# Sparse attention loop: TensorE's matmuls written in one fixed order, with a lag of two pieces and the projections as filling

## The chip, the cores and the metric

The kernel runs on one core of a Trainium2 chip. The metric is the device time of one execution in microseconds (us), lower is better; the time of a kernel is the median of its runs. The engines are called as in the profile: PE (TensorE), DVE (VectorE), ACT (ScalarE), POOL (GpSimd) and SP (SyncE, which issues most DMAs).

## The reference, cut to what matters

The program is two transformer blocks in float32 on 512 tokens of width 1024. The change touches the attention of the first block's second layer: 16 heads of 64 in 4 groups that share keys and values, and three branches per head (compressed, selected and window) that are weighted by gates and added. With 512 tokens all 8 blocks are selected and the window reaches back over all tokens, so the selected and window branches are both plain causal attention, with different keys and values.

```python
def nsa_attention(q, gates, k_cmp, v_cmp, k_sel, v_sel, k_win, v_win, rel_bias):
    ...
        p_c = jax.nn.softmax(logit_c, axis=-1) * has_any[None, :, None, None, None]
        o_c = jnp.einsum('bqghn,bngd->bqghd', p_c.astype(v_cmp.dtype), v_cmp)
        ...
        p_s = jax.nn.softmax(logit_s, axis=-1)
        o_s = jnp.einsum('bqghk,bqgkd->bqghd', p_s.astype(vs.dtype), vs)
        ...
        p_w = jax.nn.softmax(logit_w, axis=-1)
        o_w = jnp.einsum('bqghk,bkgd->bqghd', p_w.astype(vw.dtype), vw)
        o = gt[..., 0:1] * o_c + gt[..., 1:2] * o_s + gt[..., 2:3] * o_w
...
    return o.reshape(B, S, N_HEADS * HEAD_DIM) @ w_o
```

## The kernel before

Every float32 operand is split into a high and a low part, and a product is three matmuls (high by high, high by low, low by high). The weights stream in as chunks of 512 KB in a fixed order (`Stream`). `take` hands out the next 128x128 tile; at every fourth tile `pre` asks for what is three half chunks ahead: a load on SP's queue (`w`), the high part on ACT (`whi`), and the low part (`wlo`) from DVE, POOL or, where an earlier stage left it in DRAM (`dlo`), by one more load on SP's queue. The buffers are 2 for `w` and 4 for each part, so a load waits until the matmuls of an older half chunk are done.

`nsa` is the attention. Its loop goes over 32 *pieces*: piece n is head n // 2, and the selected branch if n is even, the window branch if it is odd. Each piece has two halves:

- `br_a` makes the scores in four blocks of query rows (`s`, 512, 384, 256 and 128 columns wide, two matmuls each, in 2 banks). DVE adds the bias and takes the minimum, ACT takes the exponential, and at the end DVE makes a factor per row and POOL multiplies the four blocks by it (`pa`, `pb`, `pc`).
- `br_b` turns the weights in three *turns* of 4, 3 and 3 transposes (`pt`, 2 banks); after each, ACT makes the high part `ph` and DVE the low part `pl`, and the *products* with the values follow (`o`, two matmuls per key block).

Each head ends with `cmp_b`, the compressed branch (4 transposes, ACT `ct`, one product, then ACT and DVE `of`, and after the second head of a pair ACT `oh` and DVE `ol`). Between the pieces stands *filling*, a generator per group of 8 pieces (`fill`). In groups 0 to 2 it holds the next group's key and value projection (`kvsteps`), its query projection (`qsteps`) and its compressed scores (`cmp_a`, matmuls `mm<-q,kz`); group 0 first has the compression of keys and values (`phi`, matmuls `mm<-whi,eh`, a small product with much weight). In group 3 it holds the output projection of the first heads (`w_o`, matmuls `mm<-oh,whi`, `mm<-ol,whi`, `mm<-oh,wlo`). The projections' ends work on DVE and ACT: `kvsteps` makes `kf`, `vf`, two `kl` and `vv`, `qsteps` two `qf` and four `q`. The keys are copied to the other half of the partitions by four DMAs on SP's queue (`kh`, `kl`) before the first score matmul.

The program text runs `br_b` three pieces behind `br_a` (`LAG`) and takes 4, 2 or 1 steps of filling per piece (`RATE`). It is not the order on the engines: a scheduler in the kernel's framework takes the text's order as a priority and lists each engine's instructions by when its own costs say that they are ready. Each engine then runs its list in order and waits for semaphores.

## Time and profile before

| | |
|---|---|
| median of 3 runs | 2427.35 us (2426.93 to 2428.57) |
| the profiled execution, its own time | 2430.19 us |
| its span, first to last instruction | 2428.4 us |
| mean granted clock of PE | 0.991 |
| attention loop, with the end of the output projection | from about 613 to 915 us of the span |

The profile records every instruction of one execution. A busy share counts the time in which an engine has at least one instruction open; PE's instructions overlap, so that its pace is better read from the distance between the starts of two matmuls. PEld is PE's loading of weights. Times in the rows are us from the start of the span, means of a group are in ns.

### The profile page before, as it was taken

How to read it: one execution, taken by the hardware profiler on the slowest of the kernel's cores; microseconds unless marked ns; L12 is line 12 of the kernel's file. 1: busy time of each engine (PE TensorE's matmuls, PEld its weight loads, DVE VectorE, ACT ScalarE, POOL GpSimd, SP SyncE). 2: the span in 40 equal slices, each digit the busy share in tenths (PEclk: the TensorE clock that was granted, in tenths of full speed). 3: DMA queues.
4: the chain of work that ended last, by engine and by line, in shares of the span. 5: the costliest groups of instructions: out<-in, count | busy, mean ns of one | idle time of the engine just before them, and what ended most of it. 6: DMA issues, size and time to landing. Idle time of an engine off the chain costs nothing.

```text
span 2428.4 us, 38996 instructions
## 1 busy us (share of the span) xinstructions
PE 2360.5 (97%) x14369; PEld 2070.6 (85%) x14369; DVE 1644.6 (68%) x3260; ACT 1235.7 (51%) x2431; POOL 475.9 (20%) x664
## 2 busy tenths in 40 slices
PE   8999999999999989999999999999999999999997
PEld 6788888887787768888889999998989999998995
DVE  6558757765667778647658884678975567764864
ACT  4235444444777664434545775556554334432442
POOL 1231111122233331111232222123321000000001
PEclk9999999999999999999999999999999999999998
DMA  4666777776743447777766446644456262233232
GB/s 164 179 164 211 259 267 261 262 269 203 232 133 94 127 139 259 267 251 266 264 229 191 123 150 183 187 140 155 148 158 188 96 202 88 88 96 95 89 96 70
DMA packets 156396, 427.40 MB, mean 176 GB/s; under 512 B 23131, under 2 KB 29531, under 8 KB 156155
## 3 DMA queue, kind: packets, MB, share of 16 engines
q1 hardware_dynamic: 119680, 296.15, 38.2%
q0 software_dynamic: 35392, 127.49, 16.3%
q8 instruction: 113, 1.85, 0.3%
q10 hardware_dynamic: 1132, 1.26, 0.2%
q14 instruction: 79, 0.65, 0.1%
HBM read 349.01 MB, written 83.29 MB: 178 GB/s over the span
## 4 chain that ended last, share of the span: by engine, by line
PE 83%; DVE 8%; ACT 4%; DMA 3%; issue 2%; SPq 0%; DVEq 0%; ACTq 0%
PE mm L312 72%; PE g L312 3%; PE o L312 3%; DMA L<-csd 2%; PE s L312 2%; PE pt L316 1%; PE u L316 1%; DVE e L746 1%; ACT L L1566 1%; DVE cvt L1353 1%; PE u L312 1%; DVE pl L321 1%; DVE Ml L321 1%; ACT ph L320 1%; DMA w<-in_ws_dram 0%
## 5 line engine op out<-in xcount | busy, mean ns | idle before, releaser
L312 PE MATMUL mm<-hh,whi 128*128 128x258 f32 (+2 forms) x2464 | 796.1, 324 | 14.6 <-ACT hh L360 6.7
L312 PE MATMUL mm<-hh,wlo 128*128 128x258 f32 (+2 forms) x2464 | 798.5, 324 | 0.0
L312 PE MATMUL mm<-hl,whi 128*128 128x258 f32 (+2 forms) x2464 | 795.8, 323 | 2.4 <-DVE hl L361 2.4
L312 PEld LDWEIGHTS mm<-hh,whi 128*128 128x128 f32 x2464 | 464.7, 189 | 57.6 <-ACT hh L360 9.6
L312 PEld LDWEIGHTS mm<-hl,whi 128*128 128x128 f32 x2464 | 465.3, 189 | 44.1 <-DVE hl L361 3.5
L312 PEld LDWEIGHTS mm<-hh,wlo 128*128 128x128 f32 x2464 | 465.8, 189 | 38.2 <-issue 1.7
L214 ACT ACTIVATE whi<-w 128x512 fp32r<-128x512 f32 x346 | 218.3, 631 | 435.5 <-PE mm L312 334.9
L216 DVE TENSOR_TENSOR wlo<-w,whi 128x512 fp32r<-128x512 f32 x344 | 242.3, 705 | 191.7 <-ACT whi L214 184.6
L312 PE MATMUL mm<-b,whi 128*128 128x512 f32 (+1 forms) x699 | 273.5, 391 | 0.0
L312 PE MATMUL mm<-a,wlo 128*128 128x512 f32 (+1 forms) x699 | 273.5, 391 | 0.0
L312 PE MATMUL mm<-a,whi 128*128 128x512 f32 (+1 forms) x699 | 273.0, 391 | 0.0
L214 ACT ACTIVATE whi<-ax 128x512 fp32r<-128x512 f32 x154 | 97.3, 632 | 211.1 <-PE mm L312 206.2
L178 POOL DMA_DIRECT2D dlo<-al x112 | 60.5, 540 | 543.8 <-DVE al L177 414.0
L216 DVE TENSOR_TENSOR wlo<-ax,whi 128x512 fp32r<-128x512 f32 x154 | 105.9, 687 | 85.8 <-ACT whi L214 85.5
L312 PEld LDWEIGHTS mm<-b,whi 128*128 128x128 f32 x699 | 131.7, 188 | 29.8
L312 PEld LDWEIGHTS mm<-a,wlo 128*128 128x128 f32 x699 | 131.7, 188 | 29.8
L312 PEld LDWEIGHTS mm<-a,whi 128*128 128x128 f32 x699 | 131.7, 188 | 29.7
L207 ACT ACTIVATE whi<-w 128x512 fp32r<-128x512 f32 x182 | 111.8, 623 | 66.0 <-PE mm L312 59.8
L177 DVE TENSOR_TENSOR al<-aw,ah 128x1024 fp32r<-128x1024 f32 x91 | 115.9, 1273 | 25.3 <-ACT ah L176 25.3
L312 PE MATMUL mm<-oh,whi 128*128 128x258 f32 (+1 forms) x400 | 124.7, 313 | 3.0 <-ACT oh L320 2.1
L312 PE MATMUL mm<-ol,whi 128*128 128x258 f32 (+1 forms) x400 | 123.1, 308 | 0.3 <-DVE ol L321 0.3
L312 PE MATMUL mm<-oh,wlo 128*128 128x258 f32 (+1 forms) x400 | 122.8, 307 | 0.0
(540 smaller groups left out, 4450.2 us busy)
## 6 DMA issues: line engine op xcount, KB each, us to landing
w<-in_ws_dram SPq DMA_DIRECT2D x284, 512.0 KB, 3.9
aw<-in_ws_dram POOLq DMA_DIRECT2D x112, 512.0 KB, 6.1
dlo<-al POOLq DMA_DIRECT2D x112, 512.0 KB, 3.0
wlo<-dlo SPq DMA_DIRECT2D x224, 256.0 KB, 3.0
ax<-in_ws_dram SPq DMA_DIRECT2D x77, 512.0 KB, 5.7
L<-csd SPq DMA_DIRECT2D x32, 256.0 KB, 3.7
sk<-line POOLq DMA_DIRECT2D x16, 320.0 KB, 16.1
bias<-sk SPq DMA_DIRECT2D x16, 256.0 KB, 3.7
```

Of the source, the lines that this page charges most:

```text
L177: nc.vector.tensor_tensor(out=l, in0=w, in1=h.bitcast(F32), op=ALU.subtract)
L178: nc.gpsimd.dma_start(self.dlo[c], l.bitcast(F32))
L207: nc.scalar.activation(out=h[:, a], in_=src[:, a], func=AF.Copy, scale=sc)
L214: nc.scalar.activation(out=h, in_=src, func=AF.Copy)
L216: eng.tensor_tensor(out=l, in0=src, in1=h.bitcast(F32), op=ALU.subtract)
L312: self.nc.tensor.matmul(out, l, r, start=start, stop=stop)
L316: self.nc.tensor.transpose(out, in_, self.ident[0:n, 0:n])
L320: nc.scalar.activation(out=hi, in_=src, func=AF.Copy)
L321: (eng or nc.vector).tensor_tensor(out=lo, in0=src, in1=hi.bitcast(F32), op=ALU.subtract)
L746: (nc.gpsimd if g in EPOOL else nc.vector).tensor_tensor(out=ev[64 * q:64 * q + 64, :, g, 0:nn], in0=src[:, q, 4 * jh:4 * jh + 4, b:b + nn ...
L1353: nc.vector.scalar_tensor_tensor(out=t[:, s:W], in0=u[:, 0:W - s], scalar=hw(k), in1=t[:, s:W], op0=ALU.mult, op1=ALU.add)
L1566: nc.scalar.activation(out=L[:, cx * 128:cx * 128 + 128], in_=L[:, cx * 128:cx * 128 + 128], func=AF.Relu, scale=-1.0, bias=self.cs[:, cx ...
```

## The change

The loop's matmuls stand in the order of the text: PE is taken from the scheduler for the loop (`manual_schedule`); the other engines' lists are still the scheduler's, made for that order. `br_a`, `br_b`, `cmp_a` and `cmp_b` become generators that stop between their parts. Round n of the loop takes piece n's scores, piece n - 2's turns and products, the last product of piece n - 3 (`old`), and `cmp_b` of a head that is done (`c`, `late`). Three slots per round (`some`) take steps of filling, by a table: 1, 1, 2 and then 3 steps in the first ten slots (`EARLY`), after that 22, 22, 22 and 40 steps spread evenly over the 24 slots of a group (`FILL`). The generators of the filling are cut finer: one row of tiles instead of two per step, and the evacuation in a step of its own. A fifth generator (`last`) puts 6 steps of the remaining output projection, for the first two tiles of it, into the rounds after the last scores. The order around one round:

```diff
+            turn((0,))
+            yield
+            turn((1,))
+            yield
+            product(0)
+            yield
+            turn((2, 3))
+            yield
+            product(1)
+            yield
+            product(2)
+            yield
...
+        def last(ms):
+            for m in ms:
+                parts.append(mmb())
+                for k in range(KS[m], KD - 1):
+                    self.gemm([(parts[m], A)], "w_o", k * 128, m * 128, [O[k][1:]], begin=k == KS[m], end=False)
+                    yield
+
+        FILL = (22, 22, 22, 40)
+        EARLY = (1, 1, 2) + (3,) * 7
...
+        with tc.manual_schedule(engines={mybir.EngineType.PE}):
+            for n in range(35):
...
+                go(x)
+                go(y)
+                go(x)
+                some(n, 0)
+                go(old)
+                go(late)
+                go(y)
+                go(y)
+                go(x)
+                some(n, 1)
+                go(y)
+                go(y)
+                go(x)
+                go(c)
+                some(n, 2)
...
-            for k in range(0, KD, 2):
-                self.gemm_pair(ps2, [("qg", 256 * g), ("qg", 256 * g + 128)], hs, k, 2)
-                if k < 6:
-                    yield
+            for k in range(KD):
+                self.gemm_pair(ps2, [("qg", 256 * g), ("qg", 256 * g + 128)], hs, k, 1)
+                yield
```

The instructions are the same in number and shape; only their order changes. Three places show it. The first is PE's list at the loop's start, as the difference of the two programs (`s` are scores of piece 0, `mm<-whi,eh` is the compression, of which the kernel before has 25 matmuls here):

```order
 L312 MATMUL mm<-hh,wlo 128x512
 L316 MATMUL mm<-ckt,vf 128x128 x4
+L312 MATMUL s<-kh,q 128x512
+L312 MATMUL s<-kl,q 128x512
+L312 MATMUL s<-kh,q 128x384
+L312 MATMUL s<-kl,q 128x384
+L312 MATMUL mm<-whi,eh 128x256
+L312 MATMUL mm<-wlo,eh 128x256
```

The first scores moved ahead of the compression's matmuls. The second place is the end of a group. PE's list before, near the end of group 1 (no filling is left in it for four pieces):

```order
L312 MATMUL o<-ph,vv 128x512
L312 MATMUL s<-kh,q 128x256
L312 MATMUL s<-kl,q 128x256
L312 MATMUL s<-kh,q 128x512
L312 MATMUL s<-kl,q 128x512
L312 MATMUL o<-pl,vv 64x512
L312 MATMUL o<-ph,vv 128x384
L316 MATMUL pt<-ckt,pb 128x128
L316 MATMUL pt<-ckt,pa 128x128 x2
```

PE's list now, up to the next group's compressed scores (`mm<-q,kz`); six matmuls of filling stand a turn earlier:

```order
L312 MATMUL mm<-hh,wlo 128x512
L316 MATMUL pt<-ckt,pb 128x128
L316 MATMUL pt<-ckt,pa 128x128 x2
L312 MATMUL o<-ph,vv 128x384
L312 MATMUL o<-pl,vv 64x384
L312 MATMUL s<-kh,q 128x128
L312 MATMUL s<-kl,q 128x128
L316 MATMUL pt<-ckt,c_6389 96x128 x4
L312 MATMUL s<-kh,q 128x512
L312 MATMUL s<-kl,q 128x512
```

DVE's list now at the same place (`qf` and `q` are the evacuation of the query projection, `pl` the low parts that the products wait for):

```order
L920 ISA pc,mn<-s,bias 128x256
L920 ISA mn 128x1
L699 SCALAR_TENSOR_TENSOR qf<-mm,rstd 128x512 x2
L920 ISA pb,mn<-s,bias 128x128
L920 ISA mn 128x1
L706 TENSOR_TENSOR q<-qf,q 64x512 x2
L321 TENSOR_TENSOR pl<-pt,ph 128x384
L706 TENSOR_TENSOR q<-qf,q 64x512 x2
```

Filling is spread over the pieces, and the evacuation of the projections stands between the low parts of a piece. The third place is the end of the loop on PE. Before:

```order
L316 MATMUL pt<-ckt,pa 128x128
L312 MATMUL o<-ph,vv 128x512
L312 MATMUL o<-pl,vv 64x512
L316 MATMUL pt<-ckt,pb 128x128
L316 MATMUL pt<-ckt,pa 128x128 x2
L312 MATMUL o<-ph,vv 128x384
```

And now:

```order
L316 MATMUL pt<-ckt,pa 128x128
L312 MATMUL o<-ph,vv 128x512
L312 MATMUL o<-pl,vv 64x512
L312 MATMUL mm<-oh,whi 128x512
L312 MATMUL mm<-ol,whi 128x512
L312 MATMUL mm<-oh,wlo 128x512
L316 MATMUL pt<-ckt,pb 128x128
L316 MATMUL pt<-ckt,pa 128x128 x2
L312 MATMUL o<-ph,vv 128x384
```

Three matmuls of the output projection moved between the turns of the last pieces.

## Rows read from the trace of the kernel before

**Rows 1.** The page's first part: busy time of each engine, share of the span, instructions.

```profile
PE 2360.5 (97%) x14369; PEld 2070.6 (85%) x14369; DVE 1644.6 (68%) x3260; ACT 1235.7 (51%) x2431; POOL 475.9 (20%) x664
```

**Rows 2.** Busy time by stretch: the stretch, its length, then for PE, PEld, DVE, ACT and POOL the busy time and the instructions, PE's granted clock (1.00 is 2.4 GHz), the DMA engines' busy share and GB/s.

```profile
617.00:891.00 274.00, 262.66 (x1496) 214.45 (x1495) 188.34 (x531) 201.84 (x517) 94.05 (x140) 1.00 0.46 140
...
644.57:682.35 37.78, 37.38 (x204) 31.34 (x203) 25.36 (x63) 28.68 (x77) 10.66 (x17) 1.00 0.50 138
682.35:744.90 62.55, 60.45 (x345) 49.25 (x343) 45.73 (x129) 49.24 (x125) 24.35 (x36) 1.00 0.34 99
744.90:807.36 62.46, 60.13 (x342) 48.52 (x341) 45.82 (x130) 46.61 (x120) 24.08 (x37) 1.00 0.33 97
...
720.00:740.00 20.00, 19.21 (x121) 15.24 (x120) 15.78 (x51) 17.03 (x47) 8.38 (x13) 1.00 0.33 101
...
809.30:859.90 50.60, 50.57 (x275) 42.28 (x276) 31.83 (x87) 29.74 (x74) 15.49 (x22) 1.00 0.61 189
859.90:888.70 28.80, 24.73 (x150) 18.53 (x148) 19.50 (x59) 20.44 (x50) 8.71 (x12) 1.00 0.26 81
...
610.00:615.00 5.00, 2.36 (x11) 2.37 (x12) 4.46 (x9) 1.85 (x3) 0.00 (x0) 0.72 0.92 334
620.00:625.00 5.00, 3.98 (x28) 3.22 (x27) 3.37 (x12) 3.94 (x11) 0.62 (x2) 1.00 1.00 361
```

**Rows 3.** PE in order of time where it never idles: start, duration, instruction. The pace of a form is the distance from its start to the next.

```profile
855.24 0.28 PE L312 MATMUL o<-pl,vv 128*64 128x256 f32 x1
855.36 0.22 PE L312 MATMUL o<-ph,vv 128*128 128x128 f32 x1
855.42 0.22 PE L312 MATMUL o<-pl,vv 128*64 128x128 f32 x1
...
856.03 0.34 PE L312 MATMUL s<-kl,q 128*128 128x384 f32 x1
856.21 0.27 PE L316 MATMUL pt<-ckt,pc 128*128 128x128 f32 x1
856.32 0.27 PE L316 MATMUL pt<-ckt,pb 128*128 128x128 f32 x1
...
858.04 0.39 PE L312 MATMUL mm<-ol,whi 128*128 128x512 f32 x1
858.27 0.40 PE L312 MATMUL mm<-oh,wlo 128*128 128x512 f32 x1
```

**Rows 4.** PE in order of time in a stretch without filling: the first score matmul of three pieces that follow each other.

```profile
727.20 0.40 PE L312 MATMUL s<-kh,q 128*128 128x512 f32 x1
...
732.26 0.50 PE L312 MATMUL s<-kh,q 128*128 128x512 f32 x1
...
737.22 0.40 PE L312 MATMUL s<-kh,q 128*128 128x512 f32 x1
```

**Rows 5.** Groups of DVE's instructions from 646.9 to 888.7 us, shapes kept apart: count, then busy us and mean ns of one, then idle time before and what ended it.

```profile
L321 DVE TENSOR_TENSOR pl<-pt,ph 128x512 fp32r<-128x512 f32 x29 | 19.9, 686 | 4.9 <-ACT ph L320 4.8
...
L707 DVE TENSOR_TENSOR q<-qf,q 64x512 fp32r<-64x512 f32 x12 | 9.8, 819 | 0.4
...
L321 DVE TENSOR_TENSOR kl<-kf,kh 64x512 fp32r<-64x512 f32 x6 | 4.1, 686 | 0.7 <-ACT kh L320 0.7
L700 DVE SCALAR_TENSOR_TENSOR qf<-mm,rstd 128x512 f32<-128x512 f32 x6 | 4.1, 686 | 0.7 <-PE mm L312 0.7
```

**Rows 6.** PE in order of time at the end of group 1: the matmuls of the compressed scores, with the idle time before one and its releaser in brackets.

```profile
744.90 0.63 PE L312 MATMUL mm<-q,kz 128*128 128x512 f32 x2
...
746.88 1.45 PE L312 MATMUL mm<-q,kz 128*128 128x512 f32 x4 [0.26 <-DVE q L707]
```

**Rows 7.** PE in order of time at the loop's start.

```profile
612.64 1.12 PE L316 MATMUL mm<-ckt,vf 128*128 128x128 f32 x4 [3.87 <-DVE vf L823]
...
614.41 0.41 PE L312 MATMUL mm<-wlo,eh 128*128 128x256 f32 x1
614.62 0.41 PE L312 MATMUL mm<-whi,el 128*128 128x256 f32 x1
...
617.42 0.57 PE L312 MATMUL s<-kh,q 128*128 128x512 f32 x2
...
618.89 0.39 PE L312 MATMUL mm<-wlo,eh 128*128 128x256 f32 x1 [0.50 <-DMA wlo<-dlo]
```

**Rows 8.** SP's issues in order of time at the loop's start.

```profile
612.67 1.16 SPq L818 DMA_DIRECT2D kh<-kh  x2
613.94 1.18 SPq L819 DMA_DIRECT2D kl<-kl  x2
615.17 0.58 SPq L903 DMA_DIRECT2D bias<-sk  x1
615.84 1.86 SPq L204 DMA_DIRECT2D wlo<-dlo  x4
```

**Rows 9.** DMA issues from 600 to 645 us: engine, count, size, and median us from issue to landing.

```profile
bias<-sk SPq DMA_DIRECT2D x4, 256.0 KB, 4.1
...
kl<-kl SPq DMA_DIRECT2D x2, 128.0 KB, 2.3
```

**Rows 10.** PE in order of time at the loop's end: the last product and the first matmul of the rest of the output projection.

```profile
886.11 0.50 PE L312 MATMUL o<-ct,vc 96*128 96x512 f32 x1
888.67 0.80 PE L312 MATMUL mm<-oh,whi 128*128 128x512 f32 x1 [2.06 <-ACT oh L320]
```

More of the change, by code (lines that the diff above doesn't have):

```diff
@@ L445, in stat2, with gemm @@
         return r
-    def gemm(self, p, key, kr0, c0, rhs, n=128):
+    def gemm(self, p, key, kr0, c0, rhs, n=128, begin=True, end=True):
         last = len(rhs) - 1
@@ L451, in gemm @@
             for i, (ph, sl) in enumerate(p):
-                self.mm(ph, wh, h[:, sl], k == 0, False)
+                self.mm(ph, wh, h[:, sl], begin and k == 0, False)
             for i, (ph, sl) in enumerate(p):
@@ L455, in gemm @@
             for i, (ph, sl) in enumerate(p):
-                self.mm(ph, wl, h[:, sl], False, k == last)
+                self.mm(ph, wl, h[:, sl], False, end and k == last)
     def gemm_pair(self, ps, specs, rhs, k0=0, kn=8):
@@ L761, in phi @@
                 self.mm3(p[:, 0:256], eh[:, o:o + 128], el[:, o:o + 128], wh, wl, j == 0, j == 15)
-                if j % 2 and j < 15:
+                if j % 2:
                     yield
@@ L934, in br_b, with turn @@
             po = PO[h]
-            for kts in ((0,), (1,), (2, 3)):
+            groups = []
+            def turn(kts):
                 pt = ptb()
@@ L945, in br_b, with product @@
                 self.split(ph[:, 0:off], pl[:, 0:off], pt[:, 0:off])
+                groups.append((segs, ph, pl))
+            def product(i):
+                segs, ph, pl = groups[i]
                 for kt, o in segs:
@@ L963, in fill0 @@
             cts.extend(self.T(F32R, "ct") for _ in range(2))
-            cmp_a(0)
+            yield from cmp_a(0)
         def fill(g):
@@ L971, in fill @@
                 yield from qsteps(g + 1, mmb)
-                cmp_a(g + 1)
+                yield from cmp_a(g + 1)
             else:
@@ L977, in fill @@
                     p = mmb()
-                    self.gemm([(p, A)], "w_o", 0, m * 128, [O[k][1:] for k in range(KS[m])])
+                    for k in range(KS[m]):
+                        self.gemm([(p, A)], "w_o", k * 128, m * 128, [O[k][1:]], begin=k == 0, end=k == KS[m] - 1)
+                        if k < KS[m] - 1:
+                            yield
                     nc.vector.tensor_tensor(out=x[:, A], in0=p, in1=x[:, A], op=ALU.add)
@@ L1009, in nsa, with some @@
-        for x, f in pend:
-            f(x)
+        parts = []
+        def last(ms):
[3 more added lines that the diff above has]
+                    self.gemm([(parts[m], A)], "w_o", k * 128, m * 128, [O[k][1:]], begin=k == KS[m], end=False)
+                    yield
+        FILL = (22, 22, 22, 40)
+        EARLY = (1, 1, 2) + (3,) * 7
+        fills = {}
+        def some(n, i):
+            if n < 32:
+                g = n // 8
+                if g not in fills:
+                    fills[g] = fill(g)
+                j = (n % 8) * 3 + i
+                if n < 8:
+                    c = EARLY[j] if j < 10 else FILL[g] * (j - 9) // 14 - FILL[g] * (j - 10) // 14
+                else:
+                    c = FILL[g] * (j + 1) // 24 - FILL[g] * j // 24
+            else:
+                g, c = 4, 1
+                if g not in fills:
+                    fills[g] = last((0, 1))
+            for _ in range(c):
+                next(fills[g], None)
@@ new lines, in nsa @@
+        prev = {}
+        go = lambda it: next(it, None)
+        heads = iter([h for h in range(16)])
+        queue = []
+        with tc.manual_schedule(engines={mybir.EngineType.PE}):
+            for n in range(35):
+                none = iter(())
+                x = br_a(*divmod(n, 2)) if n < 32 else none
+                y = br_b(*divmod(n - 2, 2)) if 2 <= n < 34 else none
+                old = prev.get("b", none)
+                late = prev.get("c", none)
+                c = none
+                if n >= 5 and queue:
+                    c = cmp_b(queue.pop(0))
+                go(x)
[13 more added lines that the diff above has]
+                some(n, 2)
+                if n < 32 and n % 8 == 7:
+                    for _ in fills[n // 8]:
+                        pass
+                prev = {"b": y, "c": c}
+                if n >= 2 and n % 2:
+                    queue.append((n - 2) // 2)
+            for c in [prev["c"]] + [cmp_b(h) for h in queue]:
+                for _ in c:
+                    pass
@@ L1011, in nsa @@
+        assert not D and len(O) == 8
         self.xs = [self.X() for _ in range(KD)]
@@ L1013, in nsa @@
             nc.sync.dma_start(self.xs[k][:, XS], xsq[k])
+        for _ in fills[4]:
+            pass
         for m in range(KD):
-            p = mmb()
-            self.gemm([(p, A)], "w_o", KS[m] * 128, m * 128, [O[k][1:] for k in range(KS[m], KD)])
+            k0 = KD - 1 if m < len(parts) else KS[m]
+            p = parts[m] if m < len(parts) else mmb()
+            self.gemm([(p, A)], "w_o", k0 * 128, m * 128, [O[k][1:] for k in range(k0, KD)], begin=m >= len(parts))
             nc.vector.tensor_tensor(out=self.xs[m][:, XS], in0=p, in1=self.xs[m][:, XS], op=ALU.add)
```

47 lines of the change are left out of this document (17 added, 30 removed).

## The prediction

> **What bounds the kernel now.** The page's first part says PE: 97% busy over the span, DVE 68%, ACT 51% [rows 1]. So a change of order can gain only where PE waits, and the stretches say where. In the loop, 617 to 891 us, PE is open for 262.66 of 274.00 us, ACT for 201.84 and DVE for 188.34 [rows 2]. That understates the loss, because PE's instructions overlap. I therefore count work at PE's pace: where it never idles, the next matmul starts 0.23 us after one of 512 columns, 0.18 after 384, 0.12 after 256, 0.06 after 128, and 0.11 after a transpose [rows 3].
>
> A piece without filling is then 2 x (0.23 + 0.18 + 0.12 + 0.06) = 1.18 us of scores, as much of products, ten transposes for 1.10, and half a compressed branch (4 x 0.11 + 0.23) / 2 = 0.34: 3.8 us. Three pieces without filling start 5.06 and 4.96 us apart [rows 4]: 1.2 us lost per piece, 0.4 per empty slot of the new order. ACT is busy 17.03 of 20 us there [rows 2]; the turns wait for ACT and DVE.
>
> A group of the middle is 8 x 3.8 = 30.4 us, filling of 16 x 6 x 0.23 = 22.1, compressed scores of 8 x 0.23 = 1.8 and eight transposes of 0.9: 55.2 us. From one group's compressed scores to the next it takes 62.55 and 62.46 us [rows 2]: 7.3 us lost in each. The first group, 644.57 to 682.35, hardly loses (busy 37.38 of 37.78). At the end, 809.30 to 859.90 is full, 859.90 to 888.70 is not.
>
> The Trainium skill's page "Trainium Kernel Development and Optimization", section Performance Expectations, says that matmul busy time is a bad measure of the distance to the limit and that weight-load busy time is a good one. The rows agree: from 720 to 740 us PE is open for 19.21 of 20 us while PEld falls to 15.24, or 76%, against 84% in the full stretch [rows 2]. By busy time alone the loop could give 11.3 us at most; by the count above it loses about twice that.
>
> **The change, part by part.** No instruction is added, so the sum is of waits that go and waits that come. PE's list was as fixed as now when it ran; what changes is what stands behind a wait.
>
> *Start of the loop.* Before, 25 matmuls of the compression cover the copy of the keys: the scores come at 617.42 [rows 7]. Now the scores stand first. The copies are issued from 612.67 and 613.94 [rows 8] and land 2.3 us after issue [rows 9], so the low keys come at about 616.2. PE is through the transposes at 613.76 [rows 7], so it stands about 2.5 us, and the first compression matmul comes at about 616.2 + 0.23 + 0.36 = 616.8. SP's queue is behind it: low weights are loaded when an older half chunk is used up, and the next such load goes out at 615.84 [rows 8]; now it waits until about 618. The loads are back to back there, DMA busy 1.00 at 361 GB/s from 620 to 625 [rows 2], and PE already waits for one at 618.89 [rows 7], so a later start means a later end, about 2 us. Beside the compression PE also does less now: by its end the old order has begun six pieces, the new one three. I take +4 us. The bounds are +1 (only part of the 2.5 us stays) and +8 (the 2 us, and the three pieces at 3.8 us that are begun later cost half their time).
>
> For the clock the row is 610 to 615 us: granted 0.72 after an idle time of 3.87 us [rows 2, 7], with 256-column matmuls 0.21 us apart [rows 7] instead of 0.12. The skill's page "TensorE: Matmul & The Clock Gate", Part 1, says that an idle array drops to 1.2 GHz and gets 2.4 GHz back by sustained work. By it, standing again at once would keep the lower clock for the next 24 matmuls, 24 x 0.09 = 2.2 us on top of the 4; no run here shows that yet.
>
> *First group.* It was full. Now the evacuations of the projections meet a PE that has six matmuls of filling at most between two turns. On DVE `kf`, `vf` and two `kl` are 4 x 0.69 = 2.8 us, two `qf` and four `q` are 2 x 0.69 + 4 x 0.82 = 4.7 us [rows 5], and the order puts them ahead of low parts that a product waits for. PE has 2.5 us of other work between its last filling and the first compressed score, then 1.8 us of those; before, these matmuls take 2.9 us from 744.90 to 746.88 + 4 x 0.23 [rows 6]. I take 1.5 us of wait for each evacuation: +3 us. Bounds 0 (all hidden) and +7.5 (nothing hidden).
>
> *The two middle groups.* The pieces without filling go, and with them 7.3 us each. What comes is late next: of 24 slots 19 have something for PE, 5 are empty at 0.4 us, 2.0 us; and the two evacuations at 1.5 us, 3.0 us. That is 5.0 us instead of 7.3, a gain of 2.3 per group: -4.6 us. Bounds: with both evacuations hidden -5.3 per group, -10.6; with none hidden 2.0 + 7.5 = 9.5, so +2.2 per group, +4.4.
>
> *Last group and end.* In the last group every slot has three or six matmuls, and no projection is evacuated. From 859.90 to 888.70 PEld is busy 18.53 us; at the full stretch's 42.28 / 50.60 that is 22.2 us of work, 6.6 lost [rows 2]. The last chain (product, ACT, DVE, ACT, 2.06 us idle [rows 10]) stays, since the first matmul after it still needs the last head. The other 4.5 us can be filled: after the last scores now stand 27 matmuls of the output projection, 6.2 us, where six stood. Counted by pieces the loss is rather larger than 6.6, so I take -5 us, with bounds -3 and -8.
>
> POOL's factors lag a whole piece and cost nothing as long as its 94.05 us of 274.00 [rows 2] stay below a piece's time, as they do by far.
>
> **Sum**: +4 + 3 - 4.6 - 5 = -2.6 us. Of the span of 2428.4 us (2430.19 for the execution) that is 0.1%; the median is 2427.35, so **2424.7 us**. The lower bounds add up to +1 + 0 - 10.6 - 8 = -17.6, 2409.8 us; the upper ones to +8 + 7.5 + 4.4 - 3 = +16.9, 2444.3 us. A measurement of this kernel can tell about 0.2% (4.9 us) from no change.
>
> **The rivals.**
>
> *The filling pays in full*, 2409.8 us. For it: DVE and ACT are at 69% and 74% of the loop on average [rows 2], the low parts have slack while filling stands between turn and product, and the pieces without filling are the one visible loss of the middle. Against it: the order puts four to six evacuations on DVE within one piece.
>
> *DVE's queue sets the pace*, slower. Place: the end of the key and of the query projection, three times each. DVE does its list in order, so the low part behind `kl` or `q` is late, and PE, whose list is fixed too, cannot take filling instead. Price: nothing hidden, +7.5 in the first group and +4.4 in the middle, with +4 and -5 for start and end: +10.9, 2438.3 us. It decides once a low part is late by more than a piece has in hand, about one operation of 0.69 us [rows 5]. For it: DVE is idle before `q` for only 0.4 us in total, it runs them in a row [rows 5]. Against it: some of them are parted by a low part in the new list.
>
> *The loss only moves*, 2427.4 us: what the middle gains, the start and the first group give back exactly, because the same ACT and DVE work must pass through the same loop.
>
> **How the numbers follow.** The forecast has 0.40 (2418 to 2431 us; of it 0.16 lies beyond 0.2% faster), full filling 0.23, DVE's queue 0.27, a mere move 0.10. Faster by over 0.2%: 0.16 + 0.23 = 0.39; within: 0.24 + 0.10 = 0.34; slower: 0.27. The range that leaves out no more than 2 in 10 is 2411 to 2438 us. It holds both signs; the forecast's own is 2418 to 2431.
>
> **What would show it.** In the profile after: at the loop's start an idle time of PE of 2 us or more ahead of the first score matmuls, released by a DMA, and the compressed scores of group 0 later than 644.57; between two groups' compressed scores about 60 us instead of 62.5; PE's waits for DVE's `pl` just after `kl` and `q`; the stretch after the last scores with PEld as in a full one. The forecast is wrong if the middle groups take 57 us or less (full filling) or 64 and more (DVE's queue), or if the start costs nothing.

## The result, and the profile after

The changed kernel takes 2451.15 us (median of 4, 2449.67 to 2452.57), the kernel before in the same comparison 2427.96 us (2426.93 to 2430.92): ratio 1.0096, 95% interval 1.0082 to 1.0110. It is 23 us slower; forecast were 2424.7 us, at most 2438. The profiled execution of after has a span of 2450.8 us.

The page's first part hardly shows it: the same matmuls, PE 96% busy instead of 97% [rows 1].

```profile
PE 2361.4 (96%) x14369; PEld 2075.0 (85%) x14369; DVE 1648.6 (67%) x3260; ACT 1237.8 (51%) x2431; POOL 477.8 (19%) x664
```

The stretches do. They are cut as in [rows 2], from the transposes of `vf` to the compressed scores of groups 0, 1, 2 and 3, to the last product of the loop, and to the next layer's first sums (columns: stretch; length, PE, PEld, DVE, ACT, POOL busy; granted clock; DMA share, GB/s). First after:

```profile
612.76:652.21 39.45, 29.34 (x162) 25.80 (x163) 17.45 (x50) 25.25 (x69) 9.18 (x14) 0.76 0.79 259
652.21:703.64 51.43, 43.56 (x239) 35.97 (x238) 29.51 (x80) 33.48 (x85) 13.04 (x20) 0.99 0.35 103
703.64:767.12 63.48, 58.33 (x329) 48.18 (x329) 44.32 (x120) 45.51 (x115) 21.80 (x32) 0.97 0.31 92
767.12:833.56 66.44, 60.27 (x341) 50.74 (x341) 46.21 (x130) 47.59 (x120) 24.42 (x36) 0.95 0.31 90
833.56:912.71 79.15, 76.02 (x448) 63.52 (x447) 55.16 (x155) 53.55 (x134) 26.88 (x38) 1.00 0.48 155
912.71:942.14 29.43, 24.43 (x85) 17.84 (x86) 20.60 (x26) 15.43 (x25) 9.12 (x9) 0.88 0.41 143
```

and the three of before that [rows 2] lacks:

```profile
612.64:644.57 31.93, 29.75 (x200) 25.94 (x200) 20.15 (x66) 27.27 (x73) 10.58 (x18) 0.95 0.92 311
807.36:886.11 78.75, 76.48 (x432) 61.79 (x431) 52.45 (x148) 50.90 (x128) 24.39 (x35) 1.00 0.49 151
886.11:914.20 28.09, 22.58 (x86) 16.72 (x87) 20.50 (x26) 16.17 (x26) 8.53 (x8) 0.94 0.47 160
```

The work in a stretch differs (the first has 200 matmuls before and 162 after), so lengths alone mislead. Over all six stretches both kernels have the same 1598 matmuls. Counting each one at PE's pace [rows 3] and taking this from the length gives what PE lost. (The paces taken here are 0.230, 0.174, 0.118 and 0.043 us for 512, 384, 256 and 128 columns and 0.099 for a transpose. By the prediction's rounded paces a loss comes out up to 2.5 us smaller per stretch, and the differences move by 0.3 at most.)

| Stretch | lost before | lost after | difference | foreseen |
|---|---|---|---|---|
| start of the loop | 8.3 | 20.4 | +12.1 | +4 (1 to 8) |
| first group | 2.2 | 11.1 | +8.9 | +3 (0 to 7.5) |
| two middle groups | 8.7 + 9.2 | 11.8 + 13.2 | +7.1 | -4.6 (-10.6 to 4.4) |
| last group to last product | 10.4 | 8.8 | -1.6 | -5 (-8 to -3) |
| last product to next layer | 8.5 | 9.9 | +1.4 | with the row above |

The sum is +27.9 us. Behind it the same code took 1514.2 us before (2428.4 - 914.2) and 1508.7 after; over all profiled executions below it takes 1507.2 to 1521.3, so these 5 us say nothing of the change. The experiments are therefore compared by the **loop's length**, from the transposes of `vf` to the last product: 273.5 us before, 300.0 after. The medians of e3 and e8 leave out one slow execution each, of 8121 and 11311 us.

What PE waited for in after, 612 to 942 us (releaser: us in total, times, longest):

```profile
PE o L312 <- DVE pl L321: 8.8, 11, 1.3
PE mm L312 <- ACT phh L320: 4.4, 2, 3.8
PE mm L316 <- DVE vf L823: 3.9, 1, 3.9
PE mm L312 <- DVE q L706: 3.8, 1, 3.8
PE pt L316 <- DVE pl L321: 3.4, 2, 1.8
...
PE mm L312 <- DMA wlo<-dlo: 2.5, 2, 2.3
...
PE mm L312 <- DVE vv L321: 1.9, 1, 1.9
```

Of these rows only the 3.9 for `vf` stood in before as long [rows 7]. The products of before waited for `pl` as often, but not as long (same view of before, 612 to 915 us):

```profile
PE o L312 <- DVE pl L321: 2.5, 9, 0.6
```

PE's instructions at the start, where [rows 7] had scores at 617.42:

```profile
615.44 0.77 PE L312 MATMUL s<-kh,q 128*128 128x512 f32 x1 [1.56 <-DMA kh<-kh]
616.49 0.77 PE L312 MATMUL s<-kl,q 128*128 128x512 f32 x1 [0.28 <-DMA kl<-kl]
...
617.69 0.41 PE L312 MATMUL mm<-whi,eh 128*128 128x256 f32 x1
617.90 0.41 PE L312 MATMUL mm<-wlo,eh 128*128 128x256 f32 x1
...
619.73 0.28 PE L312 MATMUL mm<-wlo,eh 128*128 128x256 f32 x1
619.85 0.28 PE L312 MATMUL mm<-whi,el 128*128 128x256 f32 x1
...
628.13 0.39 PE L312 MATMUL mm<-wlo,eh 128*128 128x256 f32 x1 [2.27 <-DMA wlo<-dlo]
```

PE stands for the copies, then works at half pace (0.21 us between matmuls of 256 columns instead of 0.12; the granted clock is 0.50, which is 1.2 GHz, from 612.7 to 619.5 us: *half clock* below), then stands for weights. The 3.8 us for `phh` come by way of three queues. SP, ACT and PE:

```profile
640.17 0.33 SPq L195 DMA_DIRECT2D w<-in_ws_dram  x1
```

```profile
645.96 1.70 ACT L207 ACTIVATE whi<-w,pkt 128x256 fp32r<-128x256 f32 x4 [1.93 <-DMA w<-in_ws_dram]
...
647.95 0.36 ACT L320 ACTIVATE phh<-mm 128x256 fp32r<-128x256 f32 x1
```

```profile
648.36 0.42 PE L312 MATMUL mm<-phw,phh 128*128 128x64 f32 x1 [3.83 <-ACT phh L320]
```

The weight load that SP issues at 640.17 lands at 645.87 and holds ACT's next weight split; `phh` is listed behind that split, and PE's written list has nothing that may pass. At the first group's end it is the queries. DVE, ACT and PE, between the last query matmul and the compressed scores:

```profile
697.99 1.28 DVE L699 SCALAR_TENSOR_TENSOR qf<-mm,rstd 128x512 f32<-128x512 f32 x2
...
700.79 0.68 DVE L894 TENSOR_TENSOR of<-o,of 64x512 f32<-64x512 f32 x1
...
702.17 0.69 DVE L321 TENSOR_TENSOR ol<-of,oh 128x512 fp32r<-128x512 f32 x1
702.90 2.83 DVE L706 TENSOR_TENSOR q<-qf,q 64x512 fp32r<-64x512 f32 x4
```

```profile
701.51 0.63 ACT L320 ACTIVATE oh<-of 128x512 fp32r<-128x512 f32 x1
702.04 2.57 ACT L705 ACTIVATE q<-qf 64x512 fp32r<-64x512 f32 x4
```

```profile
703.64 0.73 PE L312 MATMUL mm<-q,kz 128*128 128x512 f32 x2 [3.81 <-DVE q L706]
```

The queries wait behind a finished head's `of`, `oh` and `ol`; from `qf` to the first usable `q` it takes over 5 us, and PE's list has 1.7 us of turns, products and scores there.

### The profile page after: what moved, and what is told of

The parts are those of the page before. It is cut to its first block, busy times and chain, and to the rows that moved or that the text cites. A ratio compares the mean times of both kernels' runs of the same rounds, so it can differ in the third digit from the quotient of the medians.

```text
span 2450.8 us, 39034 instructions
## 1 busy us (share of the span) xinstructions
PE 2361.4 (96%) x14369; PEld 2075.0 (85%) x14369; DVE 1648.6 (67%) x3260; ACT 1237.8 (51%) x2431; POOL 477.8 (19%) x664
## 3 DMA queue, kind: packets, MB, share of 16 engines
q0 software_dynamic: 35392, 127.49, 16.1%
## 4 chain that ended last, share of the span: by engine, by line
PE 82%; DVE 8%; DMA 3%; ACT 3%; issue 2%; POOL 0%; SPq 0%; DVEq 0%; ACTq 0%; POOLq 0%
PE mm L312 71%; PE o L312 3%; PE g L312 3%; PE s L312 2%; DMA L<-csd 2%; PE pt L316 1%; DVE e L745 1%; DVE pl L321 1%; PE u L316 1%; PE u L312 1%; ACT L L1644 1%; DVE cvt L1431 1%; DVE Ml L321 1%; DMA w<-in_ws_dram 0%; ACT whi L207 0%
## 5 line engine op out<-in xcount | busy, mean ns | idle before, releaser
L312 PE MATMUL mm<-b,whi 128*128 128x512 f32 (+1 forms) x699 | 273.5, 391 | 0.0
L312 PE MATMUL mm<-a,wlo 128*128 128x512 f32 (+1 forms) x699 | 273.5, 391 | 0.0
```

The source lines that it names most:

```text
L312: self.nc.tensor.matmul(out, l, r, start=start, stop=stop)
```

## The experiments

Each loop's length comes from one execution, and lengths of one order differ by some 2 us. In group 2 the lists of PE, DVE, ACT and POOL are the same in after, e1, e4, e6, e10 and e14. It takes 66.4 to 66.8 us in after, e4 and e6, which fall to half clock in it, and 64.2 to 64.3 in e1, e10 and e14, which don't. So where this decides I compare the stretches.

The profiled execution of after took the longest of its four (2452.57 us), those of e10 and e14 the shortest of theirs (2448.08 and 2443.99). The ratios of e1, e5, e10, e12 and e14 lie within the interval of after's. What these five win in the loop, 2.5 to 7.1 us, is therefore a reading of their traces that the times don't confirm. The ratios of e2, e6 and all runs that are fixed from piece 8 on stand clear of after's.

In what follows a piece's number stands for the stretch from its first score matmul to that of the next piece; the turns and products in it belong to the piece two before. What such a stretch loses is counted by the paces of the table above.

| Run | loop's length, us | median, us | ratio to before (95%) |
|---|---|---|---|
| before / after | 273.5 / 300.0 | 2427.96 / 2451.15 | 1.0096 (1.0082 to 1.0110) |
| e1 compression first | 297.0 | 2452.16 | 1.0090 (1.0067 to 1.0114) |
| e2 order not fixed | 281.0 | 2435.95 | 1.0033 (1.0018 to 1.0049) |
| e3 room for q | 303.6 | 2456.30 | 1.0105 (1.0069 to 1.0140) |
| e4 no tail | 300.8 | 2454.44 | 1.0106 (1.0074 to 1.0137) |
| e5 low parts on POOL | 297.5 | 2450.48 | 1.0092 (1.0072 to 1.0112) |
| e6 fixed from piece 8 | 282.1 | 2439.20 | 1.0052 (1.0036 to 1.0069) |
| e7 e6 with e5 | 278.6 | 2435.65 | 1.0036 (1.0023 to 1.0049) |
| e8 before with POOL | 275.3 | 2427.74 | 1.0003 (0.9989 to 1.0018) |
| e9 / e11 queries first, with and without POOL | 279.0 / 288.7 | 2433.35 / 2443.32 | 1.0027 (1.0011 to 1.0043) / 1.0065 (1.0044 to 1.0085) |
| e10 kept busy | 295.0 | 2450.72 | 1.0098 (1.0068 to 1.0129) |
| e12 later products | 295.2 | 2450.62 | 1.0091 (1.0070 to 1.0112) |
| e13 e7 with e12 | 274.9 | 2431.36 | 1.0011 (0.9996 to 1.0026) |
| e14 even first group | 292.9 | 2449.31 | 1.0087 (1.0068 to 1.0106) |
| e15 e13, places moved | 274.6 | 2429.34 | 1.0001 (0.9987 to 1.0014) |
| e16 e15, high parts on POOL | 274.6 | 2428.81 | 0.9995 (0.9982 to 1.0009) |
| e17 / e18 scores put off, fixed from 8 / throughout | 279.0 / 290.7 | 2431.65 / 2444.38 | 1.0016 (1.0004 to 1.0028) / 1.0073 (1.0059 to 1.0087) |

**What is it: the fixed order, its start, its end?**

```diff
 e1
-        EARLY = (1, 1, 2) + (3,) * 7
+        EARLY = (0, 0, 0) + (3,) * 7
...
+            fills[0] = fill(0)
+            for _ in range(4):
+                next(fills[0])
             for n in range(35):
 e2
-        with tc.manual_schedule(engines={mybir.EngineType.PE}):
+        if True:
 e4
-                    fills[g] = last((0, 1))
+                    fills[g] = last(())
```

> Changed kernel, but with 24 matmuls of the compression ahead of the first scores, as the kernel before had 25; the rest of the first pieces' filling is cut by as much. Theory 'late start' (the start loses 12 us because PE stands for the copies of the keys and then for weights whose loads went out late, and runs at half clock after each): no wait for kh or kl at 613 us, low weights issued at about 616 instead of 619, first compressed scores at 645 to 648 instead of 652.2, time 2443 to 2447 us. Rival 'the order itself' (the fixed list is slow wherever the filling stands, because DVE's and ACT's parts come late to it): the first wait is saved and paid later, compressed scores at 650 or later, time 2448 to 2452 us.

> Changed kernel without the fixed order: the same generators called in the same sequence, but the scheduler lists PE's instructions as in the kernel before. Theory 'fixed places' (filling that stands at written places can't step in where DVE or ACT is late): the waits of 3.8 us for q and for phh go, groups take 60 to 62.5 us, time 2424 to 2431 us. Rival 'finer steps' (what costs is the sequence of the generators, and with it ACT's and DVE's lists): waits of 1 us and more at the same places, 2440 to 2452 us.

> Changed kernel without the part that fills the end: the 15 matmuls of the output projection that it moved behind the last scores stand behind the loop again. The prediction's term (the end gains 5 us by them): 2455 to 2457 us. Rival 'the end was hardly fillable' (the two traces give 1.3 us less lost between the last scores and the last product): 2452 to 2453 us.

By its time e1 went to the rival. One sign of the theory came: the compressed scores of group 0 stand at 647.4, 36.2 us after `vf` instead of 39.5 in after. But 2.2 of these 3.3 us are lost again up to those of group 1. The waits for the copies go, but the next scores wait 3.3 us in their place, for a bank that DVE empties late:

```profile
620.28 0.39 PE L312 MATMUL s<-kh,q 128*128 128x256 f32 x1 [3.34 <-DVE mn L920]
```

```profile
619.52 0.69 DVE L920 CUSTOM_DVE_ANT_0 pa<-s,bias 128x512 f32<-128x512 f32 x1 [2.73 <-DMA bias<-sk]
```

The bias's load now goes out behind two weight loads, at 614.97, and DVE has it 4.5 us later; in after it took 3.0 us (615.29 to 618.28). The compressed scores of group 1 come 89.8 us after `vf` instead of 90.9; the other 1.9 us come later, where nothing was changed.

e2 lies between theory and rival: 19 us of the 26.5 go with the fixed list (15 by the medians). The other 7.5 stay with the finer steps and their sequence: the scheduler now pulls filling forward (group 2's compressed scores at 729.0 instead of 744.9), and the last group, left without, loses 16.1 us up to its last scores.

e4 didn't do what was expected of it. From the compressed scores of group 3 to the last product its trace has 138 matmuls of the output projection, and 54 behind, just as after's and before's have: the scheduler put as many ahead of the last product, only 13 of them earlier. So e4 compares two places for them. Its loop is 0.8 us longer, and from the compressed scores of group 3 to the next layer it takes 108.0 us against 108.6 after and 106.8 before. Neither place gained anything on before.

**Where: the first group, or every evacuation?**

```diff
 e6
+            if n == 8:
+                man.enter_context(tc.manual_schedule(engines={mybir.EngineType.PE}))
 e5 (e8: the same in the kernel before; e7: e5 and e6)
-                    nc.vector.tensor_tensor(out=q[64 - 64 * e:128 - 64 * e], in0=src, in1=hi.bitcast(F32), op=ALU.subtract)
+                    (nc.gpsimd if g and e else nc.vector).tensor_tensor(
+                        out=q[64 - 64 * e:128 - 64 * e], in0=src, in1=hi.bitcast(F32), op=ALU.subtract)
-                self.split(hn, ln, src)
+                self.split(hn, ln, src, eng=nc.gpsimd if g else None)
```

> Changed kernel with the low parts of the later groups' keys (2 per group) and of half their queries (2 of 4) computed by POOL instead of DVE. Theory 'burst on DVE' (a row of kl and q of 1.4 to 2.8 us on DVE holds back the low parts that PE's fixed list needs next, and the clock falls on top): each of three groups loses 3 to 4 us less, the last product of the loop comes at 901 to 905 us instead of 912.7, time 2439 to 2445 us. Rival 'latency of the evacuation' (the compressed scores wait for the last q, on whatever engine; POOL takes 1.1 to 1.4 us for an operation of 512 columns against DVE's 0.7): waits for q as long or longer, last product at 911 to 916 us, 2449 to 2456 us.

> Changed kernel with the fixed order from piece 8 on only; the first group's pieces are listed by the scheduler. Theory 'most is lost in the first group' (the loop's start 12.1 and the first group 8.9 of 27.9 us): compressed scores of group 1 at 680 to 690 instead of 703.6, last product at 889 to 897 us, 2428 to 2437 us. Rival 'work put off' (what the scheduler does earlier in the first group is missing as filling at its end): last product at 905 us or later, 2443 us or more.

> Fixed order from piece 8 on, and low parts of keys and half the queries on POOL. If both theories hold the gains add up: last product at 880 to 889 us, 2419 to 2429 us, which is the kernel before or better. If POOL's latency decides: as with the fixed order from piece 8 alone or up to 4 us later.

> The kernel before with the same low parts on POOL. Theory 'burst on DVE': the two pieces around each group's end (3.7 and 1.2 us lost) lose 2 us less, three times: last product at 879 to 883 us instead of 886.1, 2421 to 2425 us. Rival: the scheduler already fills around the burst, so nothing changes: 885 to 888 us, 2426 to 2431 us.

e6 answers it: with the first group listed by the scheduler the loop is 17.9 us shorter, and the last product comes at 895.0, as the theory expected; the time, 2439.20 us, lies 2 us above the theory's range. Three of its stretches, to compare with after's second, third and fifth:

```profile
642.47:687.40 44.93, 40.51 (x220) 33.25 (x219) 27.94 (x77) 33.77 (x90) 13.56 (x21) 1.00 0.45 139
687.40:748.82 61.42, 57.13 (x322) 47.24 (x323) 43.66 (x115) 43.76 (x112) 22.48 (x32) 0.97 0.31 90
...
815.62:894.99 79.37, 76.24 (x448) 63.48 (x447) 55.07 (x155) 53.53 (x134) 26.89 (x38) 1.00 0.48 154
```

The later groups are as after's to a us or two, so two thirds of the loop's loss sit in the first group (half of the loss by the medians, 12.0 of 23.2 us). POOL gave 2.5 us (e5) and 3.5 us on top of e6 (e7), less than the theory promised (e5's time is in its rival's range, e7 lies between the two). Most of it lies in group 2 (64.1 us instead of 66.4, 63.8 instead of 66.8), where half clock lasts 3.4 us in e5 instead of 6.0 in after, and doesn't come in e7 where e6 has 6.8 us of it. In e5 the products' waits for `pl` fall from 8.8 to 4.9 us, but POOL needs 1.35 us for a low part of `q` where DVE needs 0.80 (e5's groups by line), and the compressed scores of group 1 come no earlier: 91.2 us after `vf` instead of 90.9. In the kernel before POOL brings nothing (e8).

**Is the group's end latency or capacity?**

```diff
 e3
+        S0 = EARLY + (3, 3, 2, 1, 1, 3, 3, 2, 1, 0, 0, 1, 1, 1)
+        S1 = (1, 1, 2, 1, 1, 2, 1, 0, 1, 1, 2, 1, 1, 2, 1, 1, 0, 0, 0, 1, 1, 1, 0, 0)
 e9, e11
-                yield from kvsteps(g + 1, mmb)
-                yield from qsteps(g + 1, mmb)
-                yield from cmp_a(g + 1)
+                kv, q, ca = kvsteps(g + 1, mmb), qsteps(g + 1, mmb), cmp_a(g + 1)
...
 e12 (e13: the same on e7)
                 some(n, 0)
                 go(old)
                 go(late)
                 go(y)
-                go(y)
                 go(x)
                 some(n, 1)
+                go(old)
                 go(y)
                 go(y)
```

> Changed kernel with other places of the filling in groups 0 to 2: the steps of the key and query projections stand closer, so that one empty slot more parts the values' evacuation from their transposes and three empty slots part the query evacuation from the compressed scores. Theory 'no room for the evacuation': the waits of 3.81 us (DVE q) and 1.89 us (DVE vv) and the half clock after them go, and each of three groups loses 2 to 4 us less: 2441 to 2446 us. Rival 'DVE is the bound': its list holds the same operations, so waits for pl take their place, and the empty slots cost 0.4 us each: 2449 to 2454 us.

> Fixed order from piece 8 on and low parts on POOL as in the run of both, and in addition the query projection ahead of the key projection, so that the evacuation of the queries, the compressed scores and their softmax have key matmuls as filling beside them (the compressed scores and their transposes then use the score and turn banks). Theory 'evacuations without filling beside them are what a group still loses' (10.5 us, of it some 9 in four or five pieces): 3 to 5 us less for each of two to three groups, last product at 877 to 884 us instead of 889.8, 2422 to 2430 us. Rival 'the loss moves to the key evacuation', which now stands at the group's end without filling and with its copies ahead of the next scores: last product at 888 to 893 us, 2433 to 2439 us.

> As the run with the query projection first, but all low parts on DVE. Theory 'evacuations without filling beside them': most of the gain stays, last product at 880 to 888 us. Rival 'DVE's burst is what has to go': 892 us or later.

> Changed kernel, fixed order throughout, but each value product stands one place later in its piece (the first behind two places of filling instead of one, the second and third in the next piece), so that ACT and DVE have more time for the parts of a turn. Theory 'too little room between turn and product' (the waits for pl are latency): the 8.8 us of product waits for pl fall under 2 us, each group from 1 on loses 3 to 6 us less, last product at 896 to 905 us instead of 912.7. Rival 'ACT and DVE have no time in those pieces' (the waits are capacity): the waits show up at the turns, which need a bank that a late pl holds, last product at 909 to 915 us.

> The same later products in the kernel with the fixed order from piece 8 on and low parts on POOL. Theory 'room': last product at 876 to 884 us instead of 889.8, that is ahead of the kernel before (886.1), 2418 to 2428 us. Rival 'capacity': 887 to 892 us, 2432 to 2438 us.

e3 went to the rival, and 2 us beyond its range: the waits for `q` and `vv` go (`vv` to 1.0 us in three), but the empty places cost more; piece 6, without filling, now waits 4.0 us for `of`, and pieces 13 and 21, where the queries are evacuated, lose 5.0 and 5.6 us. e9 went to its rival too, level with e7; without POOL (e11) it is 9.7 us worse, so a burst on DVE does cost where the key evacuation stands bare at the end. (e9 and e11 compute part of the output wrongly, for a cause that was not found. Their matmuls are the same in number, so their times are used for the order alone.) e12 split the theories. Its waits, same stretch and columns as above:

```profile
PE s L312 <- DVE mn L920: 3.9, 3, 2.0
PE mm L312 <- DVE vv L321: 3.8, 3, 2.1
PE pt L316 <- ACT ct L884: 3.8, 2, 2.0
...
PE o L312 <- DVE pl L321: 2.6, 2, 1.3
```

The products' waits for `pl` fall from 8.8 to 2.6 us, as the theory 'room' says. But new ones stand at the turns, the scores and the projection (`ct`, `mn`, `vv`), which wait for banks that late work holds, as the rival says. On balance 4.8 us of the loop are won here. 2.3 of them lie in group 2, as much as e1, e10 and e14 win there with after's own lists, so they may be the clock alone. e13 wins 3.7 us over e7, and neither has half clock in that group; with 887.5 for the last product it still goes to the rival.

**The first group again, and the clock**

```diff
 e14
-                    c = EARLY[j] if j < 10 else FILL[g] * (j - 9) // 14 - FILL[g] * (j - 10) // 14
+                    c = 47 * (j + 1) // 24 - 47 * j // 24
 e10
+        def warm(b, n):
+            for _ in range(n):
+                self.mm(b, hs[0][0][:, 16:144], hs[0][0][:, XS], True, True)
```

> Changed kernel, fixed order throughout, with the 47 steps of filling of the first group spread evenly, 2 to a place, instead of 3 to a place for the compression. Theory 'late weights' (the fixed order asks for the compression's weights faster than the late loads bring them, and PE stands 2.3 us for a load and 3.8 us for a part of phh behind a weight split on ACT): both waits go, the three pieces 1 to 3 lose 8 to 11 us instead of 17.7, last product at 903 to 908 us. Rival 'the chain of the compression' (its own turns, activation and split have no other work beside them): the waits stay in size and only move, 910 to 915 us.

> Changed kernel with 29 matmuls of 512 columns that compute nothing of use (their bank is overwritten), 5 ahead of the first scores, 12 ahead of the products of phh with phw where PE waited 3.83 us, 12 ahead of the compressed scores of group 1 where it waited 3.81 us. They lie inside the waits, so only the clock can change. Theory 'the clock makes each wait dearer' (37.5 us of the loop at half clock instead of 6.8 in the kernel before): half clock falls to 17 to 27 us, last product at 905 to 909 us instead of 912.7. Rival 'the waits alone are the loss' (ACT and DVE set the pace after a wait, so a faster PE waits again): last product at 911 to 914 us.

e14, with the compression at 2 steps a place, is 7.1 us shorter, 5.6 of it up to the compressed scores of group 1: pieces 1 to 3 lose 10.2 us instead of 17.7, the wait for `wlo` falls to 1.2 us and that for `phh` to 1.2. So by its trace some 6 us go with the compression's pace, as the theory 'late weights' says, though both waits only shrink. The other part lies in group 2, 2.2 us shorter with the same lists as in after.

e10 is 5.0 us shorter though it does more: 1.4 us up to group 1's compressed scores, 1.4 in group 1, and 2.2 in group 2, which it leaves alone and which is as much shorter in e1 and e14 without any added matmuls. It also reached two of its three places only: the five matmuls meant for the wait ahead of the first scores ran over 20 us earlier,

```profile
578.81 1.09 PE L312 MATMUL s<-hh 128*128 128x512 f32 x4
```

and half clock stayed there (612.5 to 622.7). At the other two places the added matmuls lie in the waits. The granted clock (last column but two), first after, then e10, in the same two stretches:

```profile
646.90:653.70 6.80, 5.34 (x18) 4.75 (x19) 2.38 (x9) 5.00 (x19) 2.75 (x4) 0.50 0.39 151
704.90:708.30 3.40, 3.40 (x11) 2.60 (x11) 0.80 (x2) 1.07 (x2) 0.42 (x2) 0.50 0.00 0
```

```profile
646.90:653.70 6.80, 5.42 (x30) 4.28 (x28) 2.38 (x7) 5.41 (x18) 2.95 (x6) 1.00 0.54 175
704.90:708.30 3.40, 3.40 (x23) 2.81 (x22) 1.72 (x7) 1.58 (x5) 0.42 (x2) 1.00 0.07 8
```

After two waits of 3.8 us, PE in after worked at the lower of its two levels, 1.2 GHz. (Of e10's 30 matmuls in the first stretch 8 are added ones, in the second none.) What this costs shows in the instructions from `phh` to the compressed scores of group 0, the same ones in both: in after they begin at 648.36 (above) and the scores at 652.21, 3.85 us later, in e10 1.92 us later:

```profile
652.21 2.70 PE L312 MATMUL mm<-q,kz 128*128 128x512 f32 x8
```

```profile
648.37 0.19 PE L312 MATMUL mm<-phw,phh 128*128 128x64 f32 x1
...
650.29 2.03 PE L312 MATMUL mm<-q,kz 128*128 128x512 f32 x8
```

In all some 37 us of after's loop and its end are at that level, 7 of before's and 20 of e10's. The Trainium skill's page "TensorE: Matmul & The Clock Gate", Part 1, says that an idle array drops to 1.2 GHz; these rows agree. The gain didn't last, though: e10's ratio, 1.0098, is no better than after's.

**A version that beats both?** e15 to e18 put the remedies together on e13.

```diff
 e15
+        S1 = (1,) * 10 + (0,) + (1,) * 9 + (0,) + (1,) * 3
 e16, on e15
+                    if g and e:
+                        nc.gpsimd.tensor_copy(hi, src)
+                    else:
...
 e17, on e13 with e16's high parts; e18 the same, fixed throughout
+            else:
+                yield from cmp_a(g)
...
-                yield from cmp_a(g + 1)
```

> Kernel with the fixed order from piece 8 on, low parts on POOL and later products, and in addition two of a group's empty places moved: one behind the values' transposes (the query projection waited 1.59 us there for their bank), one between the query evacuation and the compressed scores. Theory 'latency' (with the right places the rest of the waits goes too): pieces 11 and 19 lose 1 us instead of 2.2, pieces 15 and 23 1.5 instead of 2.3 to 2.6, last product at 882 to 885.5 us, before the 886.1 of the kernel before, 2422 to 2428 us. Rival 'capacity' (ACT and DVE have these operations to do in these pieces wherever PE's filling stands): last product at 886.5 to 889 us, 2429 to 2434 us.

> As the run with room again, with the high parts of half the later groups' queries on POOL as well, which takes two operations of some 0.64 us from ACT in each group. If ACT's list is what is left (a turn waited 2.0 us for ct there): pieces 15 and 23 lose another 1 us less, last product at 880 to 884 us. If the latency of the query evacuation is: the compressed scores wait for POOL and the last product comes 1 to 3 us later than in the other run.

> Kernel with the fixed order from piece 8 on, part of the low and high parts on POOL and later products, and in addition the compressed scores of a group put off into the first piece of that group (its heads need them only four pieces later), so that the evacuation of the queries has the turns of a whole piece ahead of the scores. Theory 'latency': pieces 7 and 8 lose 3 to 5 us instead of 9.5, the ends of groups 1 and 2 1 us less, last product at 878 to 882 us against 886.1 in the kernel before, 2418 to 2424 us, ratio to the kernel before 0.996 to 0.999. Rival 'capacity': the operations of DVE and ACT meet in piece 8 instead of 7, last product at 884 to 888 us, 2426 to 2431 us.

> The same with the fixed order over all pieces, so that the two differ by the first group's order alone. Theory 'first group' (its written order costs 17 us whatever is done later): last product 14 to 20 us later than in the run with the scores deferred, 2434 to 2442 us. Rival 'the remedies work in the first group too': less than 8 us later.

e15 and e16 reach the kernel before (ratios with 1 in the interval) and don't pass it; e15's 887.7 for the last product is in its rival's range, and e16's loop is no shorter. In e16 pieces 11 and 19 still lose 2.0 us, 14 to 16 and 22 to 24 1.2 to 2.0 each, and 7 with 8, where the scheduler's list meets the fixed one, 9.5. e17 took 1.4 us from these two and gave more back in pieces 12 and 20 (3.1 and 4.6): the wait moves, and the last product, at 891.5, comes later than both theory and rival had it. e18 is 11.7 us longer than e17, between theory and rival: the first group's written order costs that much with the other remedies in.

## Why the prediction was wrong, step by step

The step that failed is the price of a wait in a written list: 1.5 us for each evacuation, about 2 us for all the weights that come late at the start, and no lower clock behind either. The runs show 1.9 us for `vv`, 3.8 for `q`, 2.3 for `wlo` and 3.8 for `phh` in single waits, with half clock after three of these. The whole sum was -2.6 us; by the table above it is +27.9 (23 us in the time). Every term came out higher than foreseen, the middle groups by most.

- **Start of the loop, +4 foreseen, +12.1 measured.** The mechanism came as foreseen (first scores wait for the copies, 1.8 us instead of 2.5; the low weights' loads go out at 618.99 instead of about 618), but by e1 it is worth 1 us of net time. The size came from what follows and was missing: a written list stands at each late weight, at 628.13 for `wlo` and at 648.36 for `phh` behind ACT's late split, and after each of these waits PE runs at half clock (629.8 to 636.6 and 646.9 to 653.7). The Trainium skill's rule on the clock (page "TensorE: Matmul & The Clock Gate", Part 1) stood beside the sum; the 1.9 us that it cost behind `phh` show that it belonged in it. The start had its losses before as well: the prediction says that the loop loses "about twice" 11.3 us, while the table has 39 from `vf` to the last product (31 by the prediction's own paces), 8.3 of them at the start, which it didn't count.
- **First group, +3 foreseen, +8.9 measured**, beyond the bound of 7.5. "1.5 us of wait for each evacuation" is the mis-sized term: `vv` cost 1.89, `of` behind it 1.20 and `q` 3.81 us. I priced the evacuation's own operations. Its latency is longer, over 5 us for `q`, since that is listed behind a head's end on two engines.
- **Middle groups, -4.6 foreseen, +7.1 measured.** This turned the sign. One half held: pieces with full filling lose only some 0.35 us (piece 17: 8.00 us for 7.64 of work; the unfilled ones of before lost 1.2 [rows 4]). The other failed: pieces 11 and 19 (key evacuation) lose 3.1 and 4.2 us, the pairs 15 with 16 and 23 with 24 (queries, compressed scores and their softmax) 7.4 and 5.0. The softmax's DVE operations I hadn't counted at all.
- **Last group and end, -5 foreseen, -0.3 measured.** To the last product 1.6 us were won, behind it 1.4 lost, with clock 0.88 instead of 0.94. The term took it that matmuls from behind the loop would fill 4.5 us of waits. None came from there: 138 matmuls of the output projection stand ahead of the last product and 54 behind it, before as after; some only stand later. Why the clock is lower behind it stays open.
- **The rivals.** 'DVE's queue sets the pace' was the nearest: right place at the groups' ends, right releaser (`pl`, `q`), 63.5 and 66.4 us between groups where it says 64 and more. Its 2438.3 us were too low, because it had the start at +4 (12.1 measured), the end at -5 (-0.3) and no clock. It had a chance of 0.27 and yet lay at the very end of the stated range, 2438. The traces of e5 and e12 show that it is not DVE alone: with fewer waits for `pl`, others for ACT's parts and for banks take their place. 'The filling pays in full' and 'the loss only moves' fall with the 23 us, though the best versions, e15 and e16, end where the second of them had put the change.

What is shown, by traces and times alike: 19 of 26.5 us (15 by the medians) go with the fixed list (e2), 17.9 (12.0) with the first group's (e6), and 11.7 (12.7) with the first group's when the other remedies are in (e18 against e17). By the traces alone: some 6 us go with the compression's pace (e14), 3 with the clock behind the two waits that e10 filled, and 2 with the clock in group 2. These overlap and don't add up. What makes up the rest of the first group was not tried one by one. The trace of e14 still has waits there of 1.7 us for the copies, 1.2 for `wlo`, 1.2 for `phh`, 1.6 for `vf`, 1.2 for `of` and 2.9 for `q`; the copies' wait is worth little, since e1 took it away for 1.1 us. It also stays open whether the 1 to 2 us that the evacuation pieces still lose in e16 are latency or the capacity of ACT and DVE there: the waits changed their names in every run that gave them room.

## What to carry to other kernels

An order written for one engine is only as good as the lists of the engines that feed it: before fixing it, follow each part that it will wait for through the queues of all its producers, with what stands ahead of it there, and leave that latency as distance, not the part's own duration. Average busy shares of 70% say nothing about a piece in which three evacuations meet. Where loads and evacuations bunch, let the scheduler choose, or write the slack in, and add the half clock after a wait to the wait's price (here 1.9 us on top of 3.8).

## What the runs showed of the hardware that was not expected

The same wait need not have the same price. In group 1 all engines' lists are the same in after and e14. In after PE waits 1.81 us ahead of a turn of piece 15 and then works at half pace, in e14 1.80 us at the same place and then at full pace:

```profile
765.94 0.30 PE L316 MATMUL pt<-ckt,pb 128*128 128x128 f32 x1 [1.81 <-DVE pl L321]
...
766.33 0.67 PE L312 MATMUL s<-kh,q 128*128 128x384 f32 x1
766.80 0.52 PE L312 MATMUL s<-kl,q 128*128 128x384 f32 x1
```

```profile
761.28 0.30 PE L316 MATMUL pt<-ckt,pb 128*128 128x128 f32 x1 [1.80 <-DVE pl L321]
...
761.66 0.42 PE L312 MATMUL s<-kh,q 128*128 128x384 f32 x1
761.92 0.33 PE L312 MATMUL s<-kl,q 128*128 128x384 f32 x1
```

The next matmul starts 0.47 us later in the one and 0.26 in the other, and the piece loses 5.6 and 4.0 us. So loops of one order differ by a us or two between executions. What decides whether such a wait brings the lower clock, no run here shows.
